# Four buffer rings for a row of attention scores, loads by halves, and x ahead of weights: one decoder layer on one core

## The chip, the cores and the metric

The kernel runs on one core of a Trainium2 chip. The metric is device time in microseconds of one execution. Five engines work side by side, each through its own list of instructions in order: TensorE (PE, with its weight loads as PEld), VectorE (DVE), ScalarE (ACT), GpSimd (POOL) and SyncE (SP), whose list here holds nearly all DMA issues.

## What is computed

One layer of a decoder, 1024 tokens, width 2048, float32. Cut to what matters:

```
h   = rmsnorm(x, g_pre)
u   = h @ W_in            # q, k, v of both head groups, their gates, a low-rank forget gate
# 4 GLA heads: chunked gated linear attention, head norm, times silu(gate)
# 8 stick-breaking heads, width 128, for each block of 128 queries:
z        = (q @ k.T) * dh**-0.5
log_keep = where(s < t, log_sigmoid(-z), 0)
suffix   = reverse_cumsum(log_keep) - log_keep
w        = where(s < t, exp(log_sigmoid(z) + suffix), 0)
out      = w @ v
mix = concat(gla, sb) @ W_out
x   = x + rmsnorm(mix, g_post)
x   = x + sigmoid(x @ W_g + b_g) * (p @ W_p)
```

In the kernel the reverse sum of logarithms is a running product of sigmoid(-z), taken from the diagonal backwards.

## The kernel before, in words

Every float32 operand of a product is split into a rounded high part (ScalarE, a copy, L110) and the rest (VectorE, a subtraction, L111); a product is three matmuls: high by high, low by high, high by low. A 512-column matmul of this kind is the unit of TensorE's work. The tokens are two halves of 512 (`hf` 0 and 1); tiles are 128 partitions by 512, or by 1024 where two are held side by side.

The work goes in five stretches.

1. Entry (L434 to 463). Two products of the first quarter of x with GLA weights, eight steps of k each. Weights come as `raw` tiles, x as eight tiles `xr`, scaled by the norm's gain `g_pre` while they are split (`scaled`, L306).
2. Early products (to L540). The 16 units of GLA's q, k and v are computed by a scheme of quarter products over sums of blocks of x and of W (sets A11, A12, S1 to S4, A22, A21). Generators in `fills` load and make these sets, one step for every two steps of k. Each of the eight columns of the S2 and S1 products loads three 512 KB weights into a ring of four (`wr`), forms sums, and stores two of them (`e2_d`, `e3_d`). `norms` makes 1/rms of a half (`rstd`).
3. Attention (L549 to 1007). The loop over 24 further units of W_in (`dense`, 16 steps of six matmuls) is the filler. After each step, `step` advances the generators: `urgent` by one, `jobs` by 1.4 (RATE). `jobs` holds the four GLA heads and then `sb`, the eight stick-breaking heads; `urgent` loads q, k and v, and turns v (a transpose by DMA of 16-bit planes, `turn_by_dma`). A `yield 1` is one tick.
4. The first gate products (`small_product`), which are filler for the rest of attention; the last LAST_11 of them follow attention.
5. Gate, output and embedding products (from L1265), with wide weights `wr` and sets made by `jobs`.

A stick-breaking head has six items, each of two rows of scores (`scores`, L901); an item takes six ticks. A row is: three matmuls into one of two banks z; `kq` = sigmoid(-z) in a slot of X (L913); `sg` = sigmoid(z) in a slot of E or E2 (L914); GpSimd masks both on the diagonal (L918); VectorE's scan over kq (L924) and product into sg (L929); then `turn_by_dma` (L625): ScalarE copies sg's two 16-bit planes to a slot of X (L627), and SP issues a transposing DMA into a slot of E or E2 (L630). L1 = 8 ticks later `turned` copies both rows' pieces together (L939) and splits them into `s` and `s2`; L2 = 8 ticks after that `values` multiplies them with v. Rings, in slots: X 2, E 2, E2 2, s 2, s2 2. Even rows use E, odd rows E2, for sg and for the turned row. The turning of v takes a slot of X and one of E as well (V_MID, V_END, L634), and its copy out is L638.

The text of the kernel does not fix the order on an engine: a scheduling layer lists the instructions by priority and by its own model of when buffers come free. `tc.high_priority` moves a block ahead.

## Time and profile before

| | us |
|---|---|
| median of 3 runs | 2174.22 (2171.94 to 2176.42) |
| the profiled execution, its own time | 2171.17 |
| its span, first to last instruction | 2169.4 |
| TensorE busy | 2077.0 (96%) |
| VectorE busy | 1592.6 (73%) |
| ScalarE busy | 930.3 (43%) |
| GpSimd busy | 110.8 (5%) |

In the profile a group names line, engine, operation and tiles as out<-in, then count, busy time and mean duration, and last the idle time of the engine ahead of the group with what ended it. A wait row reads: who waited <- what ended it: us in total, times, longest. Matmuls are pipelined and their ends are modelled, so a busy TensorE can still be late. The granted clock is a share of full speed.

### The profile page before, as it was taken

To read this page: it belongs to the slowest core of one execution; us is meant where nothing else is said; L and a number is where in the kernel's file an instruction comes from. 1 tells how busy PE (TensorE), PEld (TensorE's weight loads), DVE (VectorE), ACT (ScalarE), POOL (GpSimd) and SP (SyncE) were. 2 spreads that over 40 slices of the span, in tenths; PEclk is the share of its full clock that TensorE was granted. 3 is DMA by queue.
4 is the path that set the end of the run, shared out by engine and by line. 5 is a ranking of instruction groups with operands and counts; after the bars stand their busy time and mean duration, and the time that the engine had idled before them with its cause. 6 is when DMAs were issued, how large, how long until landed. Compare 5 with 4: busy or idle time off the path is not lost.

```text
span 2169.4 us, 26781 instructions
## 1 busy us (share of the span) xinstructions
PE 2077.0 (96%) x9520; PEld 1662.7 (77%) x9520; DVE 1592.6 (73%) x2399; ACT 930.3 (43%) x1466; POOL 110.8 (5%) x228
## 2 busy tenths in 40 slices
PE   7999999999999998898899889999999999999998
PEld 6778778777777876666666668888888888778887
DVE  5777765687877766777777766788777687886765
ACT  6523432344334355666667631334324344332432
POOL 4000000000000011111111100000000000000000
PEclk9999999999999999999999999999999999999999
DMA  7888764232424135445546677898877586886763
GB/s 250 279 301 286 252 213 138 89 109 65 122 79 120 49 107 112 129 126 124 131 129 171 183 235 272 293 322 296 325 276 274 204 316 206 302 287 203 243 199 117
DMA packets 248533, 430.41 MB, mean 198 GB/s; under 512 B 126544, under 2 KB 131536, under 8 KB 248400
## 3 DMA queue, kind: packets, MB, share of 16 engines
q1 hardware_dynamic: 247824, 426.61, 60.8%
q10 hardware_dynamic: 576, 2.10, 0.3%
q8 instruction: 74, 1.21, 0.2%
q14 instruction: 59, 0.48, 0.1%
HBM read 298.09 MB, written 103.28 MB: 185 GB/s over the span
## 4 chain that ended last, share of the span: by engine, by line
PE 51%; DVE 18%; DMA 16%; ACT 7%; issue 5%; POOL 1%; SPq 1%; DVEq 0%; ACTq 0%; POOLq 0%
PE dn L99 44%; DMA E<-X 5%; PE z L99 4%; DVE X L924 3%; PE o L99 2%; DVE lo L111 2%; ACT X L627 1%; DVE E L929 1%; PE t L99 1%; DMA wr<-w_gla 1%; DMA wr<-w_gate 1%; DMA wr<-e_d 1%; ACT X L913 1%; DVE wr L210 1%; DVE wl L111 1%
## 5 line engine op out<-in xcount | busy, mean ns | idle before, releaser
L99 PE MATMUL dn<-ah,hi 128*128 128x512 f32 x1344 | 532.8, 396 | 3.8 <-ACT hi L110 3.7
L99 PE MATMUL dn<-ah,lo 128*128 128x512 f32 x1344 | 531.4, 395 | 1.6 <-DVE lo L111 1.6
L99 PE MATMUL dn<-al,hi 128*128 128x512 f32 x1344 | 531.1, 395 | 0.0
L99 PE MATMUL dn<-ah,wh 128*128 128x512 f32 x1216 | 474.6, 390 | 4.5 <-ACT wh L110 4.5
L99 PE MATMUL dn<-ah,wl 128*128 128x512 f32 x1216 | 474.3, 390 | 0.1
L99 PE MATMUL dn<-al,wh 128*128 128x512 f32 x1216 | 474.1, 390 | 0.0
L99 PEld LDWEIGHTS dn<-ah,hi 128*128 128x128 f32 x1344 | 254.5, 189 | 61.1 <-ACT hi L110 7.9
L110 ACT ACTIVATE wh<-wr 128x1024 fp32r<-128x1024 f32 x152 | 159.1, 1057 | 318.3 <-PE dn L99 144.3
L99 PEld LDWEIGHTS dn<-ah,lo 128*128 128x128 f32 x1344 | 254.6, 189 | 51.4 <-DVE lo L111 3.7
L99 PEld LDWEIGHTS dn<-al,hi 128*128 128x128 f32 x1344 | 254.7, 189 | 48.7 <-issue 0.5
L99 PEld LDWEIGHTS dn<-ah,wh 128*128 128x128 f32 x1216 | 229.1, 188 | 52.9 <-ACT wh L110 5.4
L99 PEld LDWEIGHTS dn<-ah,wl 128*128 128x128 f32 x1216 | 228.8, 188 | 48.6 <-DVE wl L111 0.7
L99 PEld LDWEIGHTS dn<-al,wh 128*128 128x128 f32 x1216 | 228.9, 188 | 47.2
L111 DVE TENSOR_TENSOR wl<-wr,wh 128x1024 fp32r<-128x1024 f32 x152 | 184.7, 1218 | 8.3 <-ACT wh L110 8.1
L213 DVE TENSOR_TENSOR wr<-wr,wr 128x1024 f32<-128x1024 f32 x64 | 78.3, 1223 | 91.3 <-DMA wr<-w_out 23.3
L924 DVE TENSOR_TENSOR_SCAN X<-X 128x128 f32<-128x128 f32 (+2 forms) x96 | 98.2, 1023 | 38.0 <-POOL X L918 30.7
L110 ACT ACTIVATE hi<-wr 128x512 fp32r<-128x512 f32 x108 | 65.6, 625 | 130.6 <-PE dn L99 74.5
L210 DVE TENSOR_TENSOR wr<-wr,wr 128x1024 f32<-128x1024 f32 x64 | 78.3, 1224 | 52.9 <-DMA wr<-w_g 29.2
L111 DVE TENSOR_TENSOR lo<-raw,hi 128x512 fp32r<-128x512 f32 x132 | 90.7, 687 | 34.5 <-ACT hi L110 33.7
L110 ACT ACTIVATE hi<-raw 128x512 fp32r<-128x512 f32 x132 | 82.7, 627 | 73.0 <-PE dn L99 64.5
L627 ACT ACTIVATE X<-E 128x256 uint16<-128x256 uint16 (+2 forms) x96 | 80.9, 843 | 63.3 <-DVE E L929 59.8
L111 DVE TENSOR_TENSOR lo<-wr,hi 128x512 fp32r<-128x512 f32 x108 | 75.4, 709 | 18.4 <-ACT hi L110 18.1
(262 smaller groups left out, 2518.5 us busy)
## 6 DMA issues: line engine op xcount, KB each, us to landing
wr<-w_g SPq DMA_DIRECT2D x64, 512.0 KB, 4.2
wr<-w_out SPq DMA_DIRECT2D x56, 512.0 KB, 4.7
wr<-w_gla SPq DMA_DIRECT2D x54, 512.0 KB, 4.3
raw<-w_in SPq DMA_DIRECT2D x96, 256.0 KB, 2.8
wr<-w_gate SPq DMA_DIRECT2D x40, 512.0 KB, 5.3
g_d<-wr SPq DMA_DIRECT2D x32, 512.0 KB, 2.9
wr<-g_d SPq DMA_DIRECT2D x32, 512.0 KB, 5.0
ar<-h_d SPq DMA_DIRECT2D x28, 512.0 KB, 4.9
```

The costliest lines, as they stand in the source:

```text
L99: PE.matmul(o, lhsT, rhs, start=start, stop=stop)
L110: A.activation(hi, src, AF.Copy)
L111: (eng or V).tensor_tensor(lo, src, f(hi), op=ALU.subtract)
L210: V.tensor_tensor(dst, a, b, op=ALU.add)
L213: V.tensor_tensor(dst, a, b, op=ALU.subtract)
L627: A.activation(pl.rearrange("p (two n) -> p two n", two=2), src.bitcast(U16)[:, :2 * n].rearrange("p (n two) -> p two n", two=2), AF.Copy)
L913: A.activation(kq[:, :n], z[:, :n], AF.Sigmoid, scale=-scale)
L924: V.tensor_tensor_scan(rev, rev, rev, initial=kq[:, n:n + 1], op0=ALU.mult, op1=ALU.bypass)
L929: V.tensor_tensor(sg[:, :n], sg[:, :n], kq[:, 1:n + 1], op=ALU.mult)
```

## The change

What it does, in parts:

- Rings of a row: kq in X (2 slots), sg in E (2), planes in X2 (2, new), turned row in E2 (3). The turning of v stays on X and E.
- q, k, v by halves: `load_gla(h, hf)` loads, scales and turns one half; it is queued at the start of the half before. `gla` waits for its own half (`loaded`) and no longer for `urgent` to be empty. `load_sb_v(h, hf)`: the second half is queued V1 = 14 ticks after the first. W1 goes from 6 to 8 ticks (the wait ahead of the transposes of k in each half of a GLA head).
- Entry: first weights and x loads at priority 1500, x ahead of the later weights.
- S1 is split from the tile in which it is made, inside `sums`; it is no longer loaded back from DRAM. `norms` waits 14 steps (first half) or none, and has three steps between its split and its column sums.
- Room: the ring `ar` goes from 3 to 2, `cw` from 1 to 2; sums of the first gate products for columns 4 to 7 go through DRAM. LAST_11 goes from 2 to 3.

```diff
-W0, W1, W2 = 3, 6, 1
+W0, W1, W2 = 3, 8, 1
-V_MID, V_END, VW = ("X", "X"), ("E", "E"), 3
+V_MID, V_END, VW, V0, V1 = "X", "E", 3, 2, 14
-LAST_11 = 2
+LAST_11 = 3
...
+            def put_1(i):
+                ones_1.append(act_wide(1, 4 + i))
+                split(*ones_1[-1], a22[i])
...
-            sets["S2"] = parts(pairs)
+            sets["S2"], sets["S1"] = parts(pairs), parts(ones_1)
...
-        def norms(hf):
-            norm_x(hf)
+        def norms(hf, wait):
+            for _ in range(wait):
+                yield 1
+            r, a, b = ep.tile([P, W], F32R, tag="xw", name=nm("xw"), bufs=3), stage(), stage()
+            hi, lo, x, y, t = [part(t, i) for t in (r, a, b) for i in range(2)][:5]
+            split(hi, lo, acc[hf])
+            for _ in range(3):
+                yield 1
+            z = ps("z")
...
-            with ahead():
+            with tc.high_priority(offset=1500):
                 w = []
...
-                dma(part(raw_x[k // 2], k), part(xT[0, k // 2], k))
+                with tc.high_priority(offset=1500):
+                    dma(part(raw_x[k // 2], k), part(xT[0, k // 2], k))
...
-        fills.extend((a12(), sums(), fill("S1", 1, 4, stored("S1"))))
+        fills.extend((a12(), sums()))
...
-        SB_BUFS = {"E2": 2, "s2": 2}
+        SB_BUFS = {"E2": 3, "s2": 2, "X2": 2}
...
+        def load_gla(h, hf):
+            k, q, *vs = heads[h]
+            k[hf], q[hf] = load_u(4 * h, hf), load_u(4 * h + 1, hf)
+            for _ in range(V0):
+                yield 1
+            V.tensor_tensor(k[hf], k[hf], rstd[hf], op=ALU.mult)
+            V.scalar_tensor_tensor(q[hf], q[hf], float(DK) ** -0.5, rstd[hf], op0=ALU.mult, op1=ALU.mult)
+            yield from load_v([(4 * h + 2 + i, hf, vs[i]) for i in range(2)], 1, True)
+            loaded.add((h, hf))
...
-                urgent.append(load_sb_v(h))
+                urgent.append(load_sb_v(h, 0))
+                at_tick(V1, lambda h=h: urgent.append(load_sb_v(h, 1)))
...
-                    tag = "E2" if qi % 2 else "E"
-                    sg = at(tag)
+                    sg = at("E")
...
-                    return turn_by_dma(sg, n, "X", tag), n
+                    return turn_by_dma(sg, n, "X2", "E2"), n
```

On ScalarE, in the third stick-breaking head, the second pair of rows of the first half. X<-z and E<-z are the two sigmoids of a row, X<-E (after: X2<-E) its planes; s and st are splits of weights and queries, hi of filler weights, u of v. Before:

```order
L913 ACTIVATE X_1648_7835<-z_1646_7828 128x384
L110 ACTIVATE s_1636_7786<-v_1635_7783 128x512
L914 ACTIVATE E_1649_7836<-z_1646_7828 128x384
L110 ACTIVATE hi_1820_8561<-raw_1819_8560 128x512
L110 ACTIVATE u_1638_7796<-o_1652_7856 128x512
L627 ACTIVATE X_1650_7846<-E_1649_7836 128x768
L913 ACTIVATE X_1654_7864<-z_1653_7860 128x512
L914 ACTIVATE E2_1655_7865<-z_1653_7860 128x512
L965 ACTIVATE o_1671_7928<-t_1588_7577 128x2x128 x2
L627 ACTIVATE X_1656_7875<-E2_1655_7865 128x1024
```

After:

```order
L927 ACTIVATE X_1643_7831<-z_1641_7824 128x384
L928 ACTIVATE E_1644_7832<-z_1641_7824 128x384
L110 ACTIVATE st_1665_7931<-u_1560_7469 128x128
L110 ACTIVATE s_1623_7737<-v_1622_7734 128x512
L110 ACTIVATE st_1666_7937<-u_1560_7469 128x128
L110 ACTIVATE hi_1729_8185<-raw_1728_8184 128x512
L927 ACTIVATE X_1648_7850<-z_1647_7846 128x512
L637 ACTIVATE X2_1645_7842<-E_1644_7832 128x768
L110 ACTIVATE s_1632_7784<-v_1631_7781 128x512
L928 ACTIVATE E_1649_7851<-z_1647_7846 128x512
L110 ACTIVATE u_1637_7800<-o_1652_7874 128x512
L637 ACTIVATE X2_1650_7861<-E_1649_7851 128x1024
```

The second row's first sigmoid now stands ahead of the first row's planes, on slots of its own.

On SP, the first DMA issues of the program: raw and wr are weights, xr is x, g_pre the gain. Before:

```order
L441 DMA raw_167<-w_gla 128x512
L441 DMA raw_173<-w_gla 128x512
L259 DMA wr_290<-w_gla 128x1024
L259 DMA wr_340<-w_gla 128x1024
L441 DMA raw_223<-w_gla 128x512
L441 DMA raw_229<-w_gla 128x512
L259 DMA wr_382<-w_gla 128x1024
L259 DMA wr_428<-w_gla 128x1024
L95 DMA c_75<-g_pre 128x16
L240 DMA lr_raw<-w_lr 128x256
L451 DMA xr_181<-xT 128x512 x2
L451 DMA xr_202<-xT 128x512 x2
```

After:

```order
L472 DMA xr_202<-xT 128x512 x2
L461 DMA raw_223<-w_gla 128x512
L472 DMA xr_235<-xT 128x512
L461 DMA raw_229<-w_gla 128x512
L472 DMA xr_235<-xT 128x512
L472 DMA xr_256<-xT 128x512 x2
L261 DMA wr_290<-w_gla 128x1024
L261 DMA wr_340<-w_gla 128x1024
L261 DMA wr_382<-w_gla 128x1024
L261 DMA wr_428<-w_gla 128x1024
L95 DMA c_75<-g_pre 128x16
L242 DMA lr_raw<-w_lr 128x256
```

Two weights and two x loads stand ahead of this piece. All x now stands ahead of the four wide weights, and g_pre behind both.

On SP again, at the end of the second product set: un_d are stores of results, wr the three weights of the next set's first columns, xw<-S1x_d the loads back of S1, e2_d and e3_d the stores of weight sums. Before:

```order
L274 DMA xw_150_836<-S1x_d1_80 128x1024
L274 DMA xw_160_874<-S1x_d2_81 128x1024
L259 DMA wr_192_1029<-w_gla 128x1024
L481 DMA un_d4_99<-raw_140_792 128x512
L274 DMA xw_170_912<-S1x_d3_82 128x1024
L481 DMA un_d6_101<-raw_151_838 128x512
L259 DMA wr_193_1031<-w_gla 128x1024
L259 DMA wr_194_1033<-w_gla 128x1024
L481 DMA un_d8_103<-raw_161_882 128x512
L495 DMA e2_d0_1009<-wr_194_1033 128x1024
```

After:

```order
L502 DMA un_d4_99<-raw_142_796 128x512
L261 DMA wr_188_1021<-w_gla 128x1024
L502 DMA un_d6_101<-raw_155_846 128x512
L261 DMA wr_189_1023<-w_gla 128x1024
L502 DMA un_d8_103<-raw_162_884 128x512
L261 DMA wr_190_1025<-w_gla 128x1024
L502 DMA un_d10_105<-raw_169_922 128x512
L261 DMA wr_201_1100<-w_gla 128x1024
L516 DMA e2_d0_1001<-wr_190_1025 128x1024
L517 DMA e3_d0_1009<-wr_188_1021 128x1024
```

The loads of S1 are gone; the third weight of the first column stands one result store later than before.

More of the change, by code (lines that the diff above doesn't have):

```diff
@@ L325, in low @@
                           start=start, stop=stop, tile_position=(0, 32 * g))
-        def norm_x(hf):
-            r, a, b = stage(dt=F32R), stage(), stage()
-            new = iter([part(t, i) for t in (r, a, b) for i in range(2)])
-            rsqrt_mean(acc[hf], D, acc[hf], lambda dt=F32: next(new))
-            rstd[hf] = acc[hf]
         raw_x = {}
@@ L527, in layer @@
         have("A11")
-        fills.extend((again("A21", 1, 0, False), norms(1)))
+        fills.extend((again("A21", 1, 0, False), norms(1, 0)))
         for j in range(8):
@@ L658, in load_sb, with load_sb_v @@
                 yield 1
-            yield from load_kq(E_GLA + 3 * h, *heads[GLA_HEADS + h][:2])
-        def load_sb_v(h):
-            yield from load_v([(E_GLA + 3 * h + 2, hf, heads[GLA_HEADS + h][2]) for hf in HALVES], 2, False)
+            k, q, _ = heads[GLA_HEADS + h]
+            for i, t in enumerate((k, q)):
+                for hf in HALVES:
+                    t[hf] = load_u(E_GLA + 3 * h + i, hf)
+            yield 1
+            loaded.add(h)
+        def load_sb_v(h, hf):
+            yield from load_v([(E_GLA + 3 * h + 2, hf, heads[GLA_HEADS + h][2])], 2, False)
         def gla(h):
-            while urgent:
-                yield 1
             kp, qp, *vp = heads[h]
@@ L881, in sb @@
                 kp, qp, vp = heads[GLA_HEADS + h]
-                while len(qp) < 2:
+                while h not in loaded:
                     yield from pause(1)
@@ L1088, in at_cw @@
     def at_cw(j):
-        if j % 2 == 0:
-            cw[0] = mt("cw", 1)
+        if j % 2 == 0 or not cw:
+            cw[0] = mt("cw", 2)
         return part(cw[0], j)
@@ L1267, in layer @@
         t2_d, t3_d = drams("g2_d", 8), drams("g3_d", 8)
-        dma2(st_u[3], u1_d)
+        for i in range(2):
+            dma2(st_u[2 + i], u1_d[i])
         for j in range(8):
```

91 lines of the change are left out of this document (45 added, 46 removed).

## The prediction

> **What bounds the kernel now.** I read the head of the page first, then a table of busy time by stage, then what TensorE waited for in the stage that loses most.
>
> ```profile
> span 2169.4 us, 26781 instructions
> PE 2077.0 (96%) x9520; PEld 1662.7 (77%) x9520; DVE 1592.6 (73%) x2399; ACT 930.3 (43%) x1466; POOL 110.8 (5%) x228
> L99 PE MATMUL dn<-ah,lo 128*128 128x512 f32 x1344 | 531.4, 395 | 1.6 <-DVE lo L111 1.6
> ```
>
> The profiled execution took 2171.17 us; its span is 2169.4. TensorE does the same matmuls before and after, so every gain has to come out of the 92 us in which it is idle, and out of two things that look busy: stretches at half clock, and the tail of a record. A record of a 512-column matmul lasts 0.395 us, but in a stage without waits one starts every 0.225 us (50 us for 222 of them, the row of 1750 below). So each wait costs about 0.17 us more than the idle time shown.
>
> The stages, in order: entry, the early products up to 360, gated linear attention (GLA) to 780, stick-breaking heads (SB) to 1270, the passage to the gate products, and as the last row a stretch of those products:
>
> ```profile
> 0.00:18.00 18.00, 6.87 (x31) 5.05 (x32) 4.67 (x9) 5.93 (x9) 0.73 (x5) 0.80 0.82 276
> 125.00:170.00 45.00, 39.68 (x158) 30.73 (x158) 33.53 (x42) 11.35 (x17) 0.00 (x0) 0.92 0.87 302
> 170.00:360.00 190.00, 188.63 (x841) 151.58 (x840) 131.38 (x192) 71.81 (x117) 0.01 (x1) 1.00 0.68 227
> 360.00:780.00 420.00, 409.57 (x2115) 329.97 (x2114) 312.45 (x643) 162.11 (x285) 17.66 (x16) 1.00 0.32 92
> 780.00:905.00 125.00, 110.59 (x497) 84.39 (x496) 88.43 (x174) 73.39 (x145) 21.63 (x54) 0.96 0.49 123
> 905.00:1270.00 365.00, 329.61 (x1540) 248.50 (x1539) 277.92 (x544) 234.16 (x452) 49.58 (x138) 1.00 0.56 144
> 1270.00:1290.00 20.00, 15.54 (x56) 12.00 (x56) 8.17 (x8) 2.66 (x4) 0.00 (x0) 0.83 0.87 309
> 1750.00:1800.00 50.00, 50.00 (x222) 41.42 (x221) 43.17 (x48) 20.46 (x20) 0.00 (x0) 1.00 0.91 320
> ```
>
> Columns: stretch, length, busy time of PE, PEld, DVE, ACT and POOL, granted clock, DMA share, GB/s. SB idles TensorE for 14.41 + 35.39 = 49.8 us, over half of all. No engine is full there: DVE is busy 366.35 of 490 us (75%). So it is a chain, not an engine. What TensorE waited for in SB:
>
> ```profile
> PE z L99 <- ACT E L914: 22.1, 30, 2.5
> PE t L99 <- DVE s L111: 10.5, 26, 0.7
> PE o L99 <- ACT s L110: 7.3, 12, 1.2
> PE t L99 <- ACT s L110: 6.0, 13, 0.7
> ```
>
> 81 waits, 45.9 us; with the tails (81 x 0.17 = 13.8 us) and the lost clock (mean 0.96 over the first 125 us, 5.0 us), 49.8 + 13.8 + 5.0 = 68.6 us can be won in SB, and TensorE's own work there is 490 - 68.6 = 421 us. The first wait is for a bank of scores that ScalarE has not read, the others for the turned weights. Why ScalarE is late:
>
> ```profile
> ACT X L627 <- DVE E L929: 59.8, 75, 2.5
> ACT E L914 <- DVE o L638: 23.6, 13, 5.5
> ACT X L913 <- DMA E<-X: 11.1, 15, 1.8
> ```
>
> ```profile
> L913 ACT ACTIVATE X<-z x96: 257/537/601, 780.7 to 1257.0; 128x512 f32<-128x512 f32 x48, 128x128 f32<-128x128 f32 x16, 128x256 f32<-128x256 f32 x16, 128x384 f32<-128x384 f32 x16
> L924 DVE TENSOR_TENSOR_SCAN X<-X 128x512 f32<-128x512 f32 x48 | 61.6, 1283 | 18.4 <-POOL X L918 11.1 <-ACT X L913 6.9
> ```
>
> The 96 rows come at 476 / 96 = 5.0 us each. A row takes two slots of X in turn (kept part, then the 16-bit planes), and X has two: the next row's first slot is free only after the product at L929, its second only when the transposing DMA has read it. Hence the rows follow each other one by one, which is the order ScalarE's list shows 96 times: sigmoid, sigmoid, planes. It stands behind the planes of one row (59.8 us for L929) while the next row's scores wait.
>
> **SB: four rings.** Kept part, sigmoid, planes and turned row get X, E, X2 and E2. The planes no longer return to X, nor turned rows to E; only V's turning still takes an X and an E. In the built order pairs of rows now overlap, and the splits move ahead: counted over the whole program, the low half of a weight split stands at most 6 matmuls ahead of its use in all 80 cases before; after, 20 stand within 5 (all in the first two heads), and the median is 33 matmuls, 33 x 0.225 = 7 us. So the waits of six heads should nearly go. The first two heads are dense: between their first scores lie 117 and 104 filler matmuls, against some 150 before. Estimate: 421 / 8 = 52.6 us of TensorE a head, less 40 fillers x 0.225 = 9, is 44; DVE has 366 / 8 = 46 a head. There DVE sets the pace; at nine tenths full, 51 us, it costs 7 us twice. I take 12 for these heads, 8 for the other six (GLA's rate: 10.4 idle in 420 us, 2.5% of 6 x 53), 4 for tails and clock: 24 left of 68.6, **-45**. Bounds: 10 left (-58); only the waits on z go, 22.1 + 30 x 0.17 = 27, less 7 new in dense heads (-20). DVE would be 366 / (421 + 24) = 82% busy; the row of 1750 holds 86% with no idle TensorE.
>
> What this clock costs is read from here:
>
> ```profile
> 792.00:796.00 4.00, 1.90 (x10) 1.31 (x10) 2.77 (x5) 1.31 (x3) 0.66 (x3) 0.99 0.76 192
> 796.00:799.40 3.40, 3.40 (x11) 2.77 (x10) 2.84 (x5) 2.03 (x4) 1.51 (x2) 0.50 0.27 60
> ```
>
> A gap of 2.1 us is followed by 3.4 us at half clock, so I keep 2 of the 4 us for one such gap in the dense heads. [...]
>
> **The entry.** Eight loads of x are moved past four 512 KB weights on SP's queue; but g_pre, without which no x can be scaled, now stands behind all of them.
>
> ```profile
> 15.87 0.72 ACT L308 ACTIVATE ah<-xr,c 128x512 fp32r<-128x512 f32 x1 [3.70 <-DMA xr<-xT]
> 17.73 0.80 PE L99 MATMUL dn<-ah,hi 128*128 128x512 f32 x1
> ```
>
> Ahead of g_pre were 3.1 MB, now 12 x 256 + 4 x 512 KB = 5.2 MB. By 18 us 276 GB/s x 18 us = 5.0 MB had moved; the rest takes one more, and landing some: about 20. Then 0.7 us for the first ah, so the first product starts near 20.7 against 17.73: **+3** (+1 to +5; the two low-rank matmuls that stood first no longer delay it). Nothing hides this: TensorE has no other work. The four weights moved back land last too, but the first of them is read only after 48 matmuls, over 10 us later.
>
> **The early products.** Four loads go (S1 is split where it is made), x tiles of the second stretch are no longer behind a weight that waits for its buffer, and the next stage's first weights are queued without those loads between.
>
> ```profile
> xw<-S1x_d SPq DMA_DIRECT2D x4, 512.0 KB, 8.4
> ```
>
> ```profile
> PE dn L99 <- ACT hi L110: 3.7, 2, 2.9
> PE dn L99 <- DVE lo L111: 1.6, 4, 0.6
> PE z L99 <- DVE xw L111: 0.8, 1, 0.8
> PE z L99 <- ACT xw L110: 0.5, 1, 0.5
> ```
>
> ```profile
> 161.00:168.00 7.00, 5.74 (x13) 4.18 (x14) 5.70 (x9) 2.19 (x4) 0.00 (x0) 0.51 0.81 310
> 1280.00:1287.00 7.00, 5.61 (x12) 4.15 (x13) 3.54 (x4) 2.00 (x2) 0.00 (x0) 0.55 0.87 307
> ```
>
> Waits on hi and lo: 5.3 us, tails 1.0, and 7 us at clock 0.51, 3.4: 9.7 in all. Four loads at 302 GB/s are 7 us of queue; the same loads otherwise remain, so I take **-7** (0 to -9.7). It falls to 0 if the chain of stores and reloads into four weight buffers, and not the four loads, set the pace there. The two waits on z are norms of x; three steps now lie between split and sum: **-1.5** (0 to -1.6). That the first norm starts 14 steps later costs nothing: its result is first read when attention begins, near 360.
>
> **GLA.** q, k, v by halves let it start after 21 steps of loads in place of 32, but W1 = 8 adds two ticks in each of eight halves (16 ticks, 11 steps): even. Its order stays as tight; 0 (-3 to +3).
>
> **The passage at 1270.** Three gate products in place of two follow the last head: 24 more matmuls, 5.4 us, while the first wide weights load. Before, this stood open:
>
> ```profile
> PE dn L99 <- ACT wh L110: 4.5, 2, 4.3
> ```
>
> With its tail and the half clock of 1280 (7 us at 0.55, 3.2) it is 8 us; 5.4 covers the 4.5, so **-7** (0 to -8). The two stores and five loads of sums that come on top lie in stages whose TensorE doesn't wait: 0; uncovered, one load costs its 4 to 5 us.
>
> Sum: 3 - 7 - 1.5 - 45 - 7 = -57.5, so 2171.17 - 57.5 = 2113.7. The profiled run lies 3 us under the median 2174.22, so I forecast **2117 us**.
>
> **Rivals.**
>
> VectorE becomes the bound in all of SB. More rows in flight bring its scans beside GpSimd's selects:
>
> ```profile
> L918 POOL TENSOR_SCALAR_AFFINE_SELECT E<-E 128x128 f32<-128x128 f32 x64 | 38.1, 595 | 81.5 <-ACT E L914 80.7
> L918 POOL TENSOR_SCALAR_AFFINE_SELECT X<-X 128x128 f32<-128x128 f32 x64 | 23.9, 373 | 48.5 <-ACT X L913 48.4
> DVE X L924 <- POOL X L918: 30.7, 57, 1.6
> ```
>
> The second select, beside a scan, takes 0.595 us against 0.373, and scans wait 30.7 us for the first. If each of 64 costs DVE half a scan, 64 x 0.64 = 41, it has 407 us; at 87% full that is 468 us of SB, -22 in place of -45: 2140. For it: the stretch. Against: the scan itself keeps its 1283 ns. Chance 0.15. [...]
>
> The transposes hold up VectorE, and it gets slower:
>
> ```profile
> DVE o L638 <- DMA E<-X: 11.7, 8, 4.0
> DVE v L939 <- DMA E<-X: 6.8, 5, 2.4
> E<-X SPq DMA_TRANSPOSE x128, 2.7
> ```
>
> A turned row is fetched by a copy in VectorE's own queue; scans and weight splits stand behind it, and weights on SP behind a blocked transpose. Thirteen waits, 18.5 us, cost 1.4 us each. If all 112 of SB did (96 rows and 16 halves of V), 366 + 157 = 523 us, 33 more than now; with +3 and no help elsewhere 2210, with the other terms 2195. It decides when a transpose costs VectorE over (490 - 366) / 112 = 1.1 us. Against: 99 of 112 cost nothing there now, a transpose lands after 2.7 us, and turned rows get three slots. Chance 0.05.
>
> The rings do little because V still borrows X and E (the 23.6 us above): with its first two heads like the others, SB wins 20 and the total is 2142. The order speaks against it, copies of V standing well ahead of the sigmoid that needs the slot. Chance 0.06. Nothing of it holds and the terms cancel, 2174: 0.03.
>
> **The numbers.** Forecast 0.71 (its own bounds 2100 to 2135), rivals 0.15, 0.05, 0.06, 0.03. From 2100 to 2150 holds more than 8 in 10, slow side included. A change under 0.2% (4 us) can't be told from none: faster 0.92, within 0.03, slower 0.05.
>
> **What would show it.** Right: waits on z and s in SB under 20 us together, planes no longer behind L929 row by row, ScalarE not waiting for a transpose, span from first to last sigmoid near 435 us; first product near 20.7; no half clock at 161 and 1280. Wrong: DVE over 90% busy with TensorE still waiting, or waits moved to copies of turned rows.

## The result, and the profile after

The changed kernel takes 2144.79 us (median; 2142.13 to 2149.54) where the kernel before takes 2173.08 on the same chip: ratio 0.9872, 95% interval 0.9847 to 0.9896. That is 28 us won; 57 were forecast. The profiled execution took 2142.80 us, 28.4 less than the one of before. Only one profiled execution of the study (that of the run e15_rotation, 2624 us at a mean granted clock of 0.72) was a slow one, and no stretch is read from it.

To see where, I number the 7680 matmuls into dn (as many in every kernel here) by their start in the trace and compare the time from one number to another, before and after. Code that no edit touches keeps most of these stretches within some 4 us from kernel to kernel of this study; 5280 to 5568 (65.9 to 71.3 us) and 6528 to 6768 (74.3 to 79.2) spread by 5.

| dn matmuls | work | before | after | won | forecast |
|---|---|---|---|---|---|
| start to first | entry | 17.7 | 20.1 | -2.4 | -3 |
| 0 to 1440 | early products | 351.8 | 342.2 | 9.6 | 8.5 |
| 1440 to 2784 | GLA | 427.6 | 426.0 | 1.6 | 0 |
| 2784 to 4128 | heads and passage | 509.2 | 477.8 | 31.4 | 52 |
| 4128 to 5280 | gate products | 261.5 | 261.4 | 0.1 | 0 |
| 5280 to 5568 | output products | 65.4 | 69.4 | -4.0 | 0 |
| 5568 to 6528 | output products | 219.3 | 219.3 | 0 | 0 |
| 6528 to 6768 | embedding begins | 71.1 | 78.7 | -7.6 | 0 |
| 6768 to last | the rest | 239.4 | 240.0 | -0.6 | 0 |

A stretch holds the same dn matmuls in every kernel, but not always as many of attention between them: by dn 2784, 891 of these have started before and 897 after. At dn 2736 it is 882 in both, and in all but one of the kernels here (e2_query_ahead). With the border there, GLA takes 412.1 us before and 409.9 after, heads and passage 524.7 and 493.9: 2.2 and 30.8 won. I call this equal work below.

The head of the page of after, and its busy time by stage (columns as before: stretch, length, PE, PEld, DVE, ACT, POOL, granted clock, DMA share, GB/s):

```profile
span 2141.1 us, 26883 instructions
PE 2060.6 (96%) x9520; PEld 1675.9 (78%) x9520; DVE 1590.4 (74%) x2399; ACT 922.9 (43%) x1466; POOL 109.1 (5%) x228
...
122.00:165.00 43.00, 43.00 (x192) 35.60 (x191) 34.08 (x42) 13.71 (x21) 0.00 (x0) 1.00 0.82 287
352.00:769.00 417.00, 409.04 (x2111) 330.00 (x2110) 310.12 (x639) 159.11 (x280) 17.42 (x16) 1.00 0.31 94
769.00:887.00 118.00, 102.80 (x478) 77.35 (x478) 96.07 (x193) 80.65 (x160) 23.57 (x62) 0.99 0.51 131
887.00:1224.00 337.00, 314.59 (x1526) 260.25 (x1526) 265.44 (x523) 217.73 (x436) 45.04 (x130) 0.98 0.61 155
865.00:1224.00 359.00, 333.08 (x1617) 274.14 (x1617) 281.70 (x557) 230.29 (x462) 49.70 (x142) 0.98 0.60 152
1816.00:1884.00 68.00, 60.09 (x243) 48.08 (x242) 56.17 (x62) 26.58 (x36) 0.00 (x0) 0.92 0.82 275
```

The stretch of early products that ran at 0.92 now runs full. The heads (769 to 1224) still idle TensorE for 15.20 + 22.41 = 37.6 us, 25.9 of them in the six later heads (from 865). At 1816 there is a new hole, 7.9 us idle at clock 0.92. What TensorE waited for in the heads, and what ScalarE waited for there:

```profile
PE z L99 <- DVE st L111: 8.8, 9, 2.5
PE z L99 <- ACT E L928: 7.5, 5, 2.6
PE z L99 <- ACT st L110: 6.4, 5, 3.0
PE t L99 <- ACT s L110: 4.8, 5, 2.4
PE t L99 <- DVE s L111: 4.4, 11, 0.7
PE o L99 <- ACT s L110: 1.6, 2, 1.4
```

```profile
ACT X L637 <- DVE E L943: 69.7, 66, 3.5
ACT s L110 <- DVE v L953: 33.9, 32, 5.2
ACT X L637 <- DMA v<-un_d: 20.2, 11, 3.3
...
ACT X L927 <- DMA E<-X: 3.2, 4, 1.0
```

The waits on weight splits (s) are down to 10.8 us from 23.8, and those on sigmoids (E) to 7.5 from 22.1. New are 15.2 us on splits of queries (st). ScalarE still stands for the product of a row (L943) 66 times: the rows are no longer chained by a slot, but its list still is.

### The profile page after: what moved, and what is told of

Read it like the earlier page. It is cut to its first block, busy times and chain, and to the rows that moved or that the text cites. A ratio compares the mean times of both kernels' runs of the same rounds, so it can differ in the third digit from the quotient of the medians.

```text
span 2141.1 us, 26883 instructions
## 1 busy us (share of the span) xinstructions
PE 2060.6 (96%) x9520; PEld 1675.9 (78%) x9520; DVE 1590.4 (74%) x2399; ACT 922.9 (43%) x1466; POOL 109.1 (5%) x228
## 3 DMA queue, kind: packets, MB, share of 16 engines
q8 instruction: 74, 1.21, 0.3%
## 4 chain that ended last, share of the span: by engine, by line
PE 59%; DVE 17%; DMA 14%; issue 5%; ACT 5%; POOL 1%; SPq 0%; ACTq 0%; DVEq 0%; POOLq 0%
PE dn L99 52%; PE z L99 3%; DMA wr<-w_g 3%; DMA v<-un_d 2%; DVE X L938 2%; PE o L99 2%; DVE wl L111 2%; DMA E<-X 1%; DVE wr L212 1%; PE t L99 1%; DVE wr L215 1%; DVE E L943 1%; DMA wr<-w_out 1%; DVE v L953 1%; DVE s L111 1%
## 5 line engine op out<-in xcount | busy, mean ns | idle before, releaser
L99 PEld LDWEIGHTS dn<-ah,hi 128*128 128x128 f32 x1344 | 254.7, 190 | 69.4 <-ACT ah L310 13.2
L215 DVE TENSOR_TENSOR wr<-wr,wr 128x1024 f32<-128x1024 f32 x64 | 78.3, 1224 | 73.4 <-DMA wr<-w_out 24.9
L212 DVE TENSOR_TENSOR wr<-wr,wr 128x1024 f32<-128x1024 f32 x64 | 78.3, 1224 | 48.8 <-DMA wr<-w_g 29.4
L938 DVE TENSOR_TENSOR_SCAN X<-X 128x128 f32<-128x128 f32 (+2 forms) x96 | 97.9, 1020 | 15.4 <-POOL X L932 14.8
L111 DVE TENSOR_TENSOR lo<-wr,hi 128x512 fp32r<-128x512 f32 x108 | 76.9, 721 | 24.3 <-ACT hi L110 23.8
```

The costliest lines, as they stand in the source:

```text
L99: PE.matmul(o, lhsT, rhs, start=start, stop=stop)
L111: (eng or V).tensor_tensor(lo, src, f(hi), op=ALU.subtract)
L212: V.tensor_tensor(dst, a, b, op=ALU.add)
L215: V.tensor_tensor(dst, a, b, op=ALU.subtract)
L938: V.tensor_tensor_scan(rev, rev, rev, initial=kq[:, n:n + 1], op0=ALU.mult, op1=ALU.bypass)
```

## The experiments

Each is the changed kernel with the edit shown; the stretches are those of the table, from one profiled execution.

### What the rings are worth, and what the halves cost

```diff
-                    sg = at("E")
+                    sg = at(tag := "E2" if qi % 2 else "E")
...
-                    return turn_by_dma(sg, n, "X2", "E2"), n
+                    return turn_by_dma(sg, n, "X", tag), n
```

> The changed kernel with one part undone: the four tiles of a row share rings as before (kept part and planes in X, sigmoid and turned row both in E or E2 by turns, two slots each); all else stays. Beside the profile of before, the changed kernel wins 20 us between the start of the stick-breaking heads and the passage. Theory A, the rings win those 20: this kernel takes 2165 us (2159 to 2170), the waits of z on the second sigmoid are back at 15 us or more and those of z on query splits fall under 5 us. Theory B, the rings win little and the halves of v do it: 2148 us (2143 to 2153).

Measured: 2177.27 us against 2168.09 before, ratio 1.0041 (1.0024 to 1.0057): the change without its rings is a loss. Heads and passage take 519.5 us against 477.8 with the rings. That is 41.7 us (38.7 by equal work); 20 lie up to dn 3936 and 21 after it. Waits in the heads, and at the passage:

```profile
PE z L99 <- ACT E L928: 16.8, 30, 1.6
```

```profile
PE dn L99 <- ACT wh L110: 12.4, 2, 12.3
```

The waits on the sigmoid are back, as theory A had it, but the price was twice what A said. The second half is the passage: here the last attention matmul stands at dn 4032 of the order, with the rings at 3960, so attention ends later against the filler, and the wide weights behind it are 12.3 us late (1.9 with the rings). The kernel falls 9 us behind the one before, although its early products take 10.8 us less; so other parts of the change cost some 20 us. Of these, 8.1 lie in 6528 to 6768 and 10.3 in heads and passage (7.9 by equal work).

Next, also what made room for the rings undone (the edit to sums of the first gate products, which no longer go through DRAM, is left out here):

```diff
-LAST_11 = 3
+LAST_11 = 2
...
-            t = keep.tile([P, W], F32, tag="ar", name=nm("ar"), bufs=2)
+            t = keep.tile([P, W], F32, tag="ar", name=nm("ar"), bufs=3)
...
-        spare = itertools.cycle((("ar", 2), ("ar", 2), ("cw", 2), ("cw", 2)))
+        spare = itertools.cycle((("ar", 3), ("ar", 3), ("ar", 3), ("cw", 1)))
```

> The changed kernel with the four rings undone, and also what made room for them: ar three slots, cw one, sums of the first gate products kept as before, LAST_11 two. Against the run with only the rings undone (2177 us, with 71 us from the 3936th to the 4128th filler matmul, 67 and 79 us in the two late stretches 5280 to 5568 and 6528 to 6768). Theory A, smaller staging and stored sums cost the late stages: these two stretches return to 65 and 71 us, and the passage to 61, the time is 2157 us (2152 to 2162). Theory B, the late loss comes from elsewhere (a shifted order that follows the new times ahead of it): the stretches stay at 67 and 79 and the time is 2170 us (2164 to 2178).

Measured: ratio 0.9992 (0.9978 to 1.0006). The stretch 6528 to 6768 goes from 79.2 to 69.9 us, so the late loss comes with the room edits. The stretch 5280 to 5568 stays (66.9, 66.6), and heads and passage take 515.3 us, still 6 more than before (3.5 by equal work). Theory A held for one of its three stretches.

The loading undone, first everywhere (with W1 back at 6), then in the stick-breaking heads alone, rings kept; of either edit the part on v:

```diff
-                urgent.append(load_sb_v(h, 0))
-                at_tick(V1, lambda h=h: urgent.append(load_sb_v(h, 1)))
+                urgent.append(load_sb_v(h))
```

> The changed kernel with q, k, v loaded whole as before (GLA and stick-breaking heads, W1 six again), the rings and all else kept. In the changed kernel GLA takes 426.0 us (1440th to 2784th filler matmul), heads and passage 477.8 us (2784th to 4128th). Theory A, the halves cost the heads and the passage 6 to 10 us: these fall to 468 to 472 us, GLA stays within 2 us, and the kernel is 6 to 10 us faster than the changed one (ratio to before 0.983 to 0.9845). Theory B, without the rings the halves cost something, but with the rings their cost is hidden: 475 to 480 us, ratio 0.986 to 0.988.

Measured: ratio 0.9859 (0.9836 to 0.9882); heads and passage 473.0 us, but GLA 430.0 in place of 426.0.

> The changed kernel with q, k, v of the stick-breaking heads alone loaded as before (both halves of v one behind the other, not 14 ticks apart); GLA keeps its halves. Theory A, what the halves cost lies in the stick-breaking heads, where the second half of v is turned in the middle of a head: heads and passage take 468 to 472 us as in the run with all halves undone. Theory B, it lies in GLA's order or nowhere: 475 us or more here.

Measured: ratio 0.9845 (0.9825 to 0.9865); heads and passage 473.7 us, GLA 425.1. Both lie between the two theories' bounds. The 430.0 us are in part a matter of the border, since 906 attention matmuls have started by dn 2784 in that run and 897 in the changed kernel. By equal work the halves win some 2 us in GLA (411.7 us undone and 412.1 before, 409.9 and 409.8 with them), and cost the heads and the passage 2.7 us by the first run (491.2 us against 493.9) and 4.9 by the second (489.0). Six profiles with the head code of the changed kernel took 491.8 to 495.3 us there, so a cost of some 3 to 5 us is likely, not certain. Against the kernel before, rings with the old loading win 524.7 - 491.2 = 33.5 us.

### Which wait holds up the six later heads

Query splits two rows ahead, in four slots; room from the turned rows' ring (three slots to two):

```diff
-  "st": 2
+  "st": 4
-        SB_BUFS = {"E2": 3, "s2": 2, "X2": 2}
+        SB_BUFS = {"E2": 2, "s2": 2, "X2": 2}
...
                     query(hf, qi + 1)
+                    query(hf, qi + 2)
```

> The changed kernel with the query splits made two rows ahead in place of one, in a ring of four in place of two (room taken from the ring of turned rows, two slots in place of three). Theory A, what is left in the six later heads is a wait by order: the split of a query stands in ScalarE's list behind the planes of an earlier row, which wait for a product on VectorE. Then the 15 us of waits of z on query splits fall under 5 us, half clock behind them goes too, and the time is 2130 us (2124 to 2138). Theory B, VectorE's load is the bound: the same 15 us turn up as waits on weight splits s or on sigmoids, and the time is 2145 us (2139 to 2151).

Measured: ratio 0.9948 (0.9928 to 0.9969), heads and passage 495.9 us. The waits on st are down to 0.2 us; these are there in their place (heads, TensorE, then VectorE):

```profile
PE z L99 <- ACT E L929: 20.8, 15, 3.3
PE t L99 <- ACT s L110: 13.5, 14, 2.4
```

```profile
DVE v L954 <- ACT X L637: 27.1, 11, 5.9
DVE v L954 <- DMA E<-X: 23.2, 23, 4.0
```

VectorE waits 23.2 us for transposes, 13.3 in the changed kernel: the third slot of turned rows is probably part of what the rings win. But the run changes two things at once, and the next takes three slots of st with the turned ring left alone (256 bytes less of DMA scratch make room too):

```diff
-  "st": 2
+  "st": 3
...
-                    kq = at("X", (P, HT + 64))[:, :HT + 1]
+                    kq = at("X", (P, HT + 8))[:, :HT + 1]
```

> The changed kernel with three slots in place of two for query splits, the ring of turned rows left at three (room from a narrower tile of kept parts, 520 columns in place of 576, and 256 bytes of DMA scratch). Query splits stay one row ahead. In the run with four query slots and two turned slots the waits on query splits went to nothing, but waits on sigmoids and weight splits took their place, and it was 15 us slower than the changed kernel. Theory A, that came from the turned slots: here the waits of z on query splits fall from 15 us to under 5 and nothing takes their place; time 2131 us (2125 to 2138). Theory B, whichever wait is removed, the next one in ScalarE's list takes over: the sum of TensorE's waits from the third head on stays over 22 us, time 2145 us (2140 to 2152).

Measured: ratio 0.9853 (0.9826 to 0.9881), heads and passage 476.8 us against 477.8. Of TensorE's waits on st 1.0 us is left, and nothing is won:

```profile
PE z L99 <- ACT E L928: 12.5, 9, 2.5
PE t L99 <- ACT s L110: 7.1, 8, 2.6
PE z L99 <- ACT b L110: 4.4, 3, 2.2
```

From 855 to 1200 the listed waits sum to 23.4 us, 26.4 from 854 to 1200 in the changed kernel. Theory B: the next in the list takes over. Then the planes a tick later:

```diff
-                    return turn_by_dma(sg, n, "X2", "E2"), n
+                    row = [None, n]
+
+                    def planes():
+                        row[0] = turn_by_dma(sg, n, "X2", "E2")
+
+                    at_tick(1, planes)
+                    return row
```

> The changed kernel with the copy of a row's planes (and its transposing DMA) issued one tick later, so that both sigmoids of both rows stand ahead of both planes in ScalarE's list. Theory A, ScalarE standing for a product (61 us of waits between 854 and 1196) with query splits and the next scores queued behind is what still makes TensorE wait: its waits on query splits and sigmoids in the six later heads fall from 19 us to under 8 and the time is 2133 us (2126 to 2139). Theory B, the waits only move, since the planes come later and so the turned row: waits on weight splits s rise by as much, and the time is 2145 us or more (2140 to 2155).

Measured: ratio 0.9844 (0.982 to 0.9868), heads and passage 474.6 us, but waits on st 16.2 us (9.7 + 6.5), as before the edit. Inconclusive: the mechanism of theory A did not show, and the interval overlaps that of the changed kernel.

A longer lead for the load of v, which had ScalarE standing 20.2 us:

```diff
             vt = load(*todo[0][:2])
-            for _ in range(3):
+            for _ in range(3 if parts == 1 else 6):
                 yield 1
```

> The changed kernel with the load of a half of v six ticks ahead of its turning in a stick-breaking head, in place of three. In the changed kernel ScalarE stands for that load 8 times, 13.6 us between 854 and 1196, with VectorE's copies of turned rows behind (17.0 us on those planes). Theory A, this standing is one of the links that keep TensorE waiting: the 13.6 us fall under 3, TensorE's waits there from 27 us to 20, the time 7 us under the changed kernel (ratio to before 0.984). Theory B, ScalarE only stands at its next wait (the product) instead: TensorE's waits stay over 24 us, ratio 0.986 to 0.988.

Measured: ratio 0.9878 (0.9848 to 0.9909), too wide to decide; heads and passage 473.1 us, 4.7 less. Six profiles with the head code of the changed kernel took 475.7 to 479.3. The same edit is in two runs below (471.0 and 472.6), but together with the planes a tick later, so some 4 us are likely and not separated from that edit. Its waits:

```profile
PE t L99 <- ACT s L110: 7.9, 10, 2.4
PE o L99 <- ACT s L110: 7.0, 8, 2.2
```

```profile
ACT X L637 <- DVE E L943: 37.2, 48, 1.9
```

ScalarE's standing for products fell by half, waits on z fell to a few us, and waits on s came. What the edit takes away is a link between two lists. The ring `v` has one slot, shared by the halves of v that are being turned and by VectorE's copies of turned rows. A copy that finds the slot taken waits until ScalarE has made the planes of v, and ScalarE waits for v to land. VectorE's waits of this kind, before, in the changed kernel and here:

```profile
DVE v L939 <- ACT X L627: 21.5, 15, 2.7
```

```profile
DVE v L953 <- ACT X L637: 27.4, 11, 4.9
```

```profile
DVE v L953 <- ACT X L637: 1.4, 3, 0.6
```

In the trace each of these waits ends with a copy of the planes of v (X<-v). In the two runs with the loading undone they are 14.0 and 17.6 us. No run here gives v a slot of its own. The last of the runs below has the same edit. TensorE still idles 33.4 us in its heads, but the waits are short (none over 1.8 us, 3.0 in the changed kernel) and the clock is full, as against 0.98 and 0.99:

```profile
765.00:1214.00 449.00, 415.56 (x1998) 326.17 (x1997) 362.56 (x715) 301.92 (x596) 67.07 (x192) 1.00 0.58 151
```

VectorE's load, first taken away, then shared:

```diff
-            split(hi[:, :n], lo[:, :n], raw[:, :n], lo_eng[turn_raw[0] % len(lo_eng)])
+            if light[0]:
+                A.activation(hi[:, :n], raw[:, :n], AF.Copy)
+                lo = hi
+            else:
+                split(hi[:, :n], lo[:, :n], raw[:, :n], lo_eng[turn_raw[0] % len(lo_eng)])
```

> The changed kernel with VectorE's subtraction for the low half of each filler weight left out while stick-breaking heads run (the high half is used twice, so TensorE's matmuls stay as many and the low half of those weights is left out of the result): about 25 subtractions of 0.69 us a head, 17 of its 44 us. Theory B, VectorE's load is the bound: TensorE's idle time from 854 to 1196 falls from 27 us to under 8 and the time to 2115 us (2108 to 2125). Theory A, order in the lists of ScalarE and VectorE: waits of z on query splits keep at least half of their 15 us, since planes still stand ahead of the splits, and the time is 2135 us (2128 to 2142).

Measured: 2125.07 us (one run), at the edge of theory B's range; heads and passage 462.9 us, 14.9 less. The expectation's count was wrong: the heads hold 64 such subtractions in the changed kernel (44.1 us), 8 a head and not 25. Waits of z on st stay at 14.8 us in the heads, as theory A had it:

```profile
PE z L99 <- DVE st L111: 8.2, 10, 1.4
PE z L99 <- ACT st L110: 6.6, 5, 2.9
```

```profile
768.00:1214.00 446.00, 416.15 (x2011) 341.96 (x2011) 327.04 (x654) 297.78 (x596) 65.77 (x192) 0.98 0.59 152
```

VectorE was busy 327.0 us there, 34.5 less than in the changed kernel (96.07 + 265.44), which is 79% of these 455 us; yet each microsecond taken off it is worth 14.9 / 34.5 = 0.4. That fits a list in order with others waiting on it better than an engine at its limit.

```diff
                 if h == 0:
                     to_sb()
+                    lo_eng[:] = [V, V, V, G]
```

> The changed kernel with every fourth subtraction for the low half of a filler weight given to GpSimd while stick-breaking heads run: some 6 to 7 of 26 a head, 4.5 us of VectorE's 44. With all of them left out the passage and the heads took 15 us less. Theory A, VectorE's load in its list counts, whoever takes it: a quarter of that, 4 us faster than the changed kernel (ratio to before 0.9855), as long as GpSimd's own takes under 5 us. Theory B, GpSimd's long operation slows VectorE beside it or holds up the weights: VectorE's scans or products grow by over 10% on average, and the kernel is slower than the changed one, ratio 0.989 or more.

Measured: ratio 0.9911 (0.9886 to 0.9937), an interval that overlaps that of the changed kernel; heads and passage 479.4 us, at the upper end of the 475.7 to 479.3 above. So nothing was won, and a loss isn't shown. GpSimd's lines:

```profile
L933 POOL TENSOR_SCALAR_AFFINE_SELECT X<-X 128x128 f32<-128x128 f32 x64 | 29.9, 467 | 108.3 <-ACT X L928 108.2
L111 POOL TENSOR_TENSOR lo<-raw,hi 128x512 fp32r<-128x512 f32 x15 | 21.7, 1445 | 47.9 <-ACT hi L110 34.1 <-DVE u L111 4.9 <-DMA u<-un_d 3.9
```

Only 15 subtractions went over, at 1445 ns each in place of VectorE's 689; the scans kept their duration (median 1190 ns, 1182 in the changed kernel), so theory B's way, slower operations on VectorE, is not shown. But its scans waited 21.0 us for GpSimd's selects in place of 14.8, so some of the 10 us taken off VectorE came back as waits. What became of the rest no run shows.

### Entry, passage and late stages

```diff
-    gpre_s = load_const(g_pre)
+    with tc.high_priority(offset=6000):
+        gpre_s = load_const(g_pre)
```

> The changed kernel with the 8 KB load of the gain g_pre put first on SyncE's queue; nothing else moves at the entry. Theory A, the late gain is what makes the entry 2.4 us slower than before: the first product starts near 13 us in place of 20.1 (two weights and two pieces of x, 1.0 MB at some 276 GB/s, behind a start of about 7 us), the 48 products then wait for x by pieces, and the time falls by 5 us, to 2140 us (2136 to 2143). Theory B, the rate of the loads sets the entry, not their order: the first product moves by under 2 us and the time stays at 2145 us (2143 to 2148).

Measured: ratio 0.9836 (0.9819 to 0.9854), 8 us under the changed kernel. The first product in the changed kernel, and with the gain first:

```profile
19.35 5.01 ACT L310 ACTIVATE ah<-xr,c 128x512 fp32r<-128x512 f32 x8 [2.97 <-DMA c<-g_pre]
...
20.12 0.79 PE L99 MATMUL dn<-ah,hi 128*128 128x512 f32 x1 [13.00 <-ACT ah L310]
```

```profile
6.03 0.72 ACT L311 ACTIVATE ah<-xr,c 128x512 fp32r<-128x512 f32 x1 [1.39 <-DMA xr<-xT]
6.80 0.50 PE L99 MATMUL dn<-ah,hi 128*128 128x512 f32 x1 [0.62 <-ACT ah L311]
```

13.3 us earlier, twice what theory A said (the start of about 7 us in its sum was an estimate that no run shows: in the changed kernel ScalarE splits the first weight from 3.80 us on); up to dn 1440, 5.7 are given back (97.2 + 250.7 against 93.8 + 248.4 us, parted at dn 384), so 7.6 stay. In the three runs below with the same edit only 3.8 to 4.3 stay: there TensorE waits 2.7 to 2.9 us for a weight near 171 us, and 3.4 to 6.8 us at half clock follow, much like the hole of before at 161. Why this run escapes it isn't shown.

```diff
-LAST_11 = 3
+LAST_11 = 2
```

> The changed kernel with LAST_11 two in place of three: two gate products in place of three follow attention. Theory A, the third product (24 matmuls, 5.4 us) is what covers the first wide weights there: the gap at the wide weights grows from 1.9 us to 7.3 us with half clock behind it, and the ratio to before goes from 0.987 to 0.990 (6 to 8 us slower than the changed kernel). Theory B, the passage won its 11 us because attention now ends earlier against the filler, by the rings: then the gap stays under 4 us and the ratio within 0.001 of 0.987.

Measured: ratio 0.9876 (0.985 to 0.9902); the gap at the wide weights is 3.1 us against 1.9, heads and passage 478.5 against 477.8. Theory B: the third product does nearly nothing that stands out of the spread.

```profile
PE dn L99 <- ACT wh L110: 3.2, 2, 3.1
```

Five staging slots, `cw` three in place of two, five names in `spare`:

> The changed kernel with five staging slots in the late stages in place of four (cw three slots in place of two). Theory A, the late stages lose 11.6 us because a load waits for a staging slot: the stretches 5280 to 5568 and 6528 to 6768 go from 69.4 and 78.7 us to 65.4 and 71.1 us, as before, and the time is 2133 us (2129 to 2138). Theory B, the loss is a matter of the order in VectorE's list there, not of slots: the stretches keep at least 68 and 76 us together, time 2143 us (2139 to 2148).

Measured: ratio 0.9839 (0.9815 to 0.9864), overlapping that of the changed kernel. 6528 to 6768 takes 75.0 us, within the 74.3 to 79.2 that twelve profiles with the rotation of the changed kernel show; so the number of slots is not it. Then the same four slots in another rotation:

```diff
-        spare = itertools.cycle((("ar", 2), ("ar", 2), ("cw", 2), ("cw", 2)))
+        spare = itertools.cycle((("ar", 2), ("cw", 2), ("ar", 2), ("cw", 2)))
```

> The changed kernel with the same four staging slots taken in another rotation (ar, cw, ar, cw in place of ar, ar, cw, cw). In the built order the first small weight of the embedding then stands in VectorE's list behind one sum fewer that waits for a store, much as before. Theory A, the rotation makes the late loss: the two late stretches go from 69.4 and 78.7 us to 66 and 72 us or less, ratio to before 0.983 (0.982 to 0.985). Theory B, the loss comes from the sums that now go through DRAM: the stretches stay within 2 us of 69 and 78.

Measured: 2135.03 to 2139.55 us in three executions, ratio 0.9834 (0.981 to 0.9859), as theory A had it. The stretches are read from one more profiled execution:

> The changed kernel with the four staging slots taken as ar, cw, ar, cw, once more, for its late stretches. In eight runs with the rotation of the changed kernel the two stretches (5280 to 5568, 6528 to 6768) together took 143 to 148 us; before, and with the old ring, 136.5. Theory A, the rotation makes the late loss: 138 us or less here. Theory B, it does not: 143 us or more.

Measured: 2132.08 us (one run); the stretches take 68.3 and 69.9 us, 138.2 together, just above theory A's bound. (The twelve profiles with the other rotation have 141.2 to 148.1, a little wider than the expectation says.) VectorE at the first small weight of the embedding, in the changed kernel and then here:

```profile
1824.55 1.23 DVE L212 TENSOR_TENSOR ar<-ar,cw 128x1024 f32<-128x1024 f32 x1
1828.16 1.23 DVE L212 TENSOR_TENSOR st<-st,ar 128x1024 f32<-128x1024 f32 x1 [2.38 <-DMA h_d<-st]
1829.30 0.42 DVE L111 TENSOR_TENSOR pl<-pr,ph 128x256 fp32r<-128x256 f32 x1
```

```profile
1821.30 1.22 DVE L212 TENSOR_TENSOR st<-st,cw 128x1024 f32<-128x1024 f32 x1
1822.44 1.22 DVE L111 TENSOR_TENSOR al<-st,ah 128x1024 fp32r<-128x1024 f32 x1
1823.57 0.42 DVE L111 TENSOR_TENSOR pl<-pr,ph 128x256 fp32r<-128x256 f32 x1
```

In the changed kernel the weight stands behind a sum that waits 2.38 us for a store to have read its tile, and TensorE behind the weight (3.0 us, the longest of three such waits). In the other rotation the sum ahead of the weight doesn't wait; VectorE's waits for a store stand elsewhere in its list (4.14 us at 1811.90, for one). That the rotation sets this stretch is shown: 69.9, 70.5 and 70.2 us in three runs with this one. The other, 5280 to 5568, is not: 65.9 to 71.3 us in eighteen profiles (the changed kernel and the edits), and I can name no edit that sets it.

### Together

Gain first, five staging slots, planes later, lead for v:

> The changed kernel with four edits together: the gain first on the queue, five staging slots, planes one tick later, six ticks of lead for v. Against the changed kernel the first alone won 8 us by the ratios (0.9836 against 0.9872), the second 7 (0.9839), the third 6 (0.9844). Theory A, they lie in different stages and add up: ratio 0.977 (0.974 to 0.980), 2122 us where before is 2172. Theory B, gains of 6 to 7 us from the second and third are mostly a new order in stages they do not touch, and do not add: ratio 0.981 to 0.984.

Measured: ratio 0.9807 (0.9783 to 0.9831), between the theories; 6528 to 6768 took 75.6 us, as it should without the other rotation.

Gain first and the other rotation:

> The changed kernel with two edits: the gain first on the queue, and the staging slots in the rotation ar, cw, ar, cw. Theory A, entry (8 us by the ratios) and late stages (8 us) are separate and add: ratio to before 0.980 (0.978 to 0.982). Theory B, they do not add: 0.983 or more.

Measured: ratio 0.9816 (0.9798 to 0.9834): 12 us under the changed kernel by the middles of the intervals, within theory A's range. In the profiled execution the two causes show in their own stretches: 3.8 us up to dn 1440, and 8.2 in 6528 to 6768.

The same with planes later and lead for v:

> As the run before (gain first, rotation ar, cw, ar, cw), and besides planes one tick later and six ticks of lead for v. Theory A, the last two take waits out of the stick-breaking heads, 4 us as the stage from the 2784th to the 4128th filler matmul showed for the lead of v alone: that stage takes 472 us, and the ratio is 0.978 (0.976 to 0.980). Theory B, waits in the heads only move: the stage stays at 476 to 478 us and the ratio is that of the run with two edits.

Measured: 2123.32 us where before takes 2170.04, ratio 0.9789 (0.976 to 0.9819), the fastest of this study; heads and passage 472.6 us, 479.3 in the run with two edits. Both are as theory A had it: planes later and lead for v together win in the heads.

## Why the prediction was right in direction and wrong in size

- **Entry, -3 forecast, -2.4 measured.** Right, and for its reason: with the gain first the first product starts 13 us earlier. That the same row said how to win, not only to lose, I did not take up.
- **Early products and norms, 8.5 forecast, 9.6 measured; no half clock at 161.** Right as a sum; not taken apart on the chip.
- **GLA, 0 forecast, 1.6 measured.** Right within its bounds. The halves do win there: some 2 us by equal work.
- **Heads, 45, and passage, 7: 52 forecast, 31.4 measured.** This is where most of the error lies. The rings' mechanism was right: without them the waits on sigmoids are back and 39 to 42 us go. The step that failed is "So the waits of six heads should nearly go", with its 8 us left. It was read from the lead of the weight splits alone, and those waits did fall. But 25.9 us stay idle in these heads, first for query splits. Taking those out as well won nothing (476.8 us), so the query ring is not the cause either, only the place where the wait showed. What the runs show in its place is links that the working left out: ScalarE stands 69.7 us for products with other work queued behind, and VectorE's copies of turned rows stand 27.4 us for the one slot of `v`. These were there before (21.5 us), but the working looked at these copies for transposes alone (6.8). With v loaded earlier they fall to 1.4 us and the stage probably wins some 4 us; the rest isn't taken apart. The two dense heads I had about right: from its first score to the next head's, VectorE is busy 40.7 of 48.2 and 38.9 of 47.6 us, with 6.2 and 5.4 us of TensorE idle (12 forecast).
- **The third gate product, by which the 7 us of the passage were argued**, won 0.7 us, less than the spread. The gap there shrank since attention now ends 43 dn matmuls earlier in the order (3960 against 4003), which the rings bring about.
- **Halves in the heads, set to nothing**, cost some 3 to 5 us; the working never priced a second half of v turned in the middle of a head.
- **Late stages, set to nothing, lost 12.** "Lie in stages whose TensorE doesn't wait: 0" failed. I priced the stores and loads that the change adds there, not that `spare` hands out its four slots in a new rotation, which moves whole rows of VectorE's list. Of the 12, 8 are that (78.7 us against 70; 4 to 9 over all profiles); the other 4 lie within a spread that no run explains.
- **Rivals.** VectorE at its limit: no, 361.51 of 455 us in the heads (79%), and scans wait 14.8 us for GpSimd, 30.7 before; but its load counts at 0.4. Transposes holding up VectorE: 13.3 us of waits, not the 1.1 us each that would decide; with two slots it begins to. First two heads like the others: no, they are the densest.
- **What would show it.** Span of the first sigmoids: 774.4 to 1206.5, 432 us (435 forecast). ScalarE's waits of a sigmoid on a transpose 11.1 to 3.2. But waits on z and s together some 37 us, not under 20, and planes behind the product 66 times. At the passage 3.4 us of half clock are left (0.52 from 1242.1). And one sign of being wrong came: VectorE's waits at copies of turned rows rose from 21.5 + 6.8 = 28.3 us to 27.4 + 13.3 = 40.7.

What stays open: which link sets the six later heads when one wait is removed after the other, why the gain put first wins 7.6 us in one run and 4 in three, and what spreads 5280 to 5568.

## What to carry to other kernels

Where several engines work through lists in order and wait for each other, a ring that breaks one link is worth only what the next link leaves: ask for every operand of the waiting matmul, not for the one with the largest wait, and for tiles of other work that take the same slot. A freed buffer is paid for somewhere, so compare the built order of the stage that gave it even where no work is added there. And look at what a small load stands behind in a queue when large ones are moved ahead of it.

## What the runs showed of the hardware

In the changed kernel the length of a gap alone doesn't tell the clock behind it: no half clock follows one of 2.41 us, and half clock follows shorter ones. Three gaps of TensorE there:

```profile
827.89 0.51 PE L99 MATMUL t<-s,u 128*128 128x256 f32 x2 [1.21 <-ACT s L110]
...
829.63 0.58 PE L99 MATMUL t<-s,u 128*128 128x256 f32 x1 [0.73 <-DVE s L111]
...
878.56 0.50 PE L99 MATMUL t<-s,u 128*128 128x256 f32 x2 [2.41 <-ACT s L110]
```

In this trace every fall and every rise of the granted clock between 30 and 2130 us lies on a grid with a step of 3.413 us. Three stretches of that grid, each with the next one (the third number from the end is the granted clock):

```profile
825.84:829.25 3.41, 1.85 (x10) 1.24 (x8) 2.68 (x5) 2.40 (x6) 1.34 (x3) 1.00 0.38 84
829.25:832.67 3.42, 3.04 (x9) 2.66 (x10) 3.42 (x7) 2.70 (x5) 1.01 (x4) 0.50 0.37 111
877.04:880.45 3.41, 1.89 (x9) 1.65 (x10) 3.22 (x6) 2.76 (x7) 0.86 (x3) 1.00 0.34 77
880.45:883.86 3.41, 2.96 (x16) 2.15 (x16) 3.41 (x7) 1.88 (x4) 1.11 (x2) 1.00 0.72 244
1054.53:1057.94 3.41, 0.89 (x6) 0.71 (x5) 3.41 (x8) 2.39 (x4) 0.56 (x3) 1.00 0.44 127
1057.94:1061.36 3.42, 3.42 (x11) 2.76 (x11) 1.53 (x5) 1.94 (x7) 0.89 (x2) 0.50 0.84 132
```

The first holds the gap of 1.21 us and the start of the one of 0.73: TensorE is idle 1.56 us, and half clock follows. The gap of 2.41 us is cut by the grid into 0.89 and 1.52, and none follows. A gap of 2.52 us (at 1057) lies whole in the third, and half clock follows. In the changed kernel the eight stretches that end in a fall hold 1.56 to 2.58 us of idle time, and the most idle one that doesn't holds 1.63; in the kernel before it is 2.03 or more against 1.52. So the border is not sharp (1.56 us with a fall, 1.63 without); with the gain first (run e4_gain_first) one fall comes after 1.36 us and none after another 1.75.

The prediction took its price of a gap from one case (2.1 us idle, then 3.4 us at half clock); by the gaps above that was too simple. Why the clock falls behind one such stretch and not behind another no run here shows.
